# Two half gates computed between FFN-out and the mixing projection, and the transposes around them rearranged

## The chip, the cores and the metric

The kernel runs on one core of one Trainium2 chip, in a single launch. The metric is the device time of one execution in microseconds, taken as the median of several runs. A core has five engines with a queue each, which they work through in order: TensorE (PE in the profile; its weight loads are PEld), VectorE (DVE), ScalarE (ACT), GpSimd (POOL) and SyncE (SP), which here only issues loads. GpSimd issues the stores.

## The reference

One layer of an encoder, with x of 1024 tokens by 1024 features, all in fp32, DFF = 2816:

```python
x = x + 0.5 * post1(swiglu_1(pre1(x)))          # FFN1: (silu(x W_g) * (x W_u)) W_out
u = pre_mix(x)                                   # RMS norm with a gain
[rq|rk|rv|rg|nq|nk|nv|g_ret|g_na] = u @ W_mix_in # widths 512 512 1024 1024 512 512 512 1024 1024
y_ret = (silu(rg) * headnorm(retention(rq, rk, rv))) @ W_ret_out   # 4 heads, chunks of 128, both directions
y_na  = (neighbourhood_attention(nq, nk, nv) + bias) @ W_na_out
x = x + post_mix((sigmoid(g_ret) * y_ret + sigmoid(g_na) * y_na) @ W_mix_out)
x = x + 0.5 * post2(swiglu_2(pre2(x)))          # FFN2
```

The gates g_ret and g_na have 1024 features each, in eight blocks of 128.

## The kernel before

**Products.** Every fp32 operand is split into a rounded high part and a remainder (`split`: ScalarE casts the high part at L60, VectorE subtracts at L61; sometimes GpSimd subtracts). `mm3` then makes three matmuls, high by high, high by low and low by high, at L87, L88 and L89. A matmul has a 128x128 stationary operand and a 128x512 moving one. `load_w` loads a 512 KB block of weights into `wraw` and splits it into two pieces, `wh` and `wl`, so it costs two casts and two subtractions. Banks of PSUM come from two rings, `ps` with six and `pt` with two.

**Token tiles.** The 1024 tokens are eight tiles of 128. The large products (FFN and mixing projection) go by 2x2 blocks in seven products instead of eight, whose operands are blocks and sums of blocks of the transposed activations: a11, a12, a21, a22 and s1 to s4. Tiles 0 to 3 give a11 and a12; tiles 4 to 7 give a21, a22 and, together with a11 and a12, s1 to s4.

**FFN-out** (`ffn_out`) runs seven products of 11 steps, in each step four token tiles of `mm3` (12 matmuls). From the fifth product on, `later.pop(0)` puts one small piece of work of tiles 0 to 3 ahead of each step. First come eight entries that finish the second halves of the outputs (`more`, each followed by an empty one), then sixteen: four stages for each of four tiles, (0) the mean square and its power on GpSimd, (1) the residual update L493 and squares, (2) the power and the normalisation L504, (3) the transposes L126 (`flip`), which write into `ps` for tiles 0 and 1 (up to the end of the sixth product, a12) and into `pt` for the others. Before, the four stages of tile 0 come first, then those of tile 1, and so on, so the transposes are the entries 4, 8, 12 and 16 of the sixteen. Tile t's halves lie in `q`. Each `flip` ends in `put`, which reads the transposed bank and writes the split operands.

**Between FFN-out and the projection.** Tiles 4 to 7 are normalised at the end of FFN-out. Their transposes are interleaved by hand with filler work for TensorE, drawn step by step (one step is one `mm3`) from the generator `first()`: 32 steps of the v projection of attention (`vproj`, the matmuls `ps<-wh,a11h` and so on), then the 24 steps of `mx.leads()`, the first products of the mixing projection. FLIP_FILL is the number of steps before each of the four flips and, last, the number between a flip and the s4 split that belongs to it. Before it asks for 40 of 56 steps, and the rest is drained afterwards. For a tile of 4 to 7, `put` does the following ring. First half (g = 0): ScalarE copies the bank to `cmb` (a21, L272), VectorE forms s3 with L276 and L277. Second half (g = 1): ScalarE casts a22h and VectorE takes a22l from the bank, VectorE adds s1 (L282), casts and subtractions for s3, VectorE subtracts the bank for s2 (L284), casts and subtractions for s1 and s2, GpSimd L287 and L288 form s4, ScalarE casts s4h and GpSimd takes s4l. `cmb` has four buffers. The evictions of the filler's v banks are `ev<-ps` on ScalarE at L1120.

**The projection.** `mx.run` takes the jobs in order; the first needs s2 of all tiles (product `ps<-s2h,wh`), whose start waits for the copy at L376.

**Later fillers.** `products()` is the generator of fillers for attention and retention: 128 steps of the v projection of retention, then the gates g_na of blocks 4 to 7 (16 steps each, both halves of the tokens), the gates g_ret, and the output projection of attention: 384 steps in all. Attention takes 148 of them (NA_FILL) and retention 234 (RET_FILL), each at a place written out by hand; what is left is drained after retention. Retention runs four heads of eight chunks. For each chunk its last step is `store`: SyncE loads a block of rg (two buffers), TensorE transposes the normalised result (L946), VectorE multiplies (L947), GpSimd issues the store to `ry` (L67). After head 3, `ry` is loaded again, split into `xy` and multiplied by W_ret_out (`ps<-xy,wh`).

These lines draw and place the filler between FFN-out and the projection, and the later gates:

```python
FLIP_FILL = (8, 8, 8, 8, 2)
def first():
    yield from vproj(wnv, ((0, 1, 2, 3),), done_nv)
    yield from mx.leads()
for f, k in zip(rest, FLIP_FILL):
    fill(k)
    f = f()
    if f is not None:
        fill(FLIP_FILL[4])
        f()
```

Of the kernel before, what the change touches and what calls it, by code (L numbers as in the profile page):

```python
# [10 lines left out]
F32 = mybir.dt.float32  # L11
F32R = mybir.dt.float32r
AF = mybir.ActivationFunctionType
# [5 lines left out]
P = 128  # L19
D = 1024  # L20
S = 1024
KT = D // P
# [6 lines left out]

NA_FILL = (12, 2, 2)  # L30
RET_FILL = (14, 2, 2, 4, 2, 3, 0, 1, 2)
FLIP_FILL = (8, 8, 8, 8, 2)
NA_UNITS = ((0, 0, 0), (3, 1, 0), (1, 0, 1), (1, 0, 2), (4, 1, 1), (4, 1, 2), (2, 0, 3), (5, 1, 3))
KEY_OFF = (0, 8, 24, 32)
RET_SCALE = 128 ** -0.5
# [499 lines left out]
def ffn_out(c, q, blocks, junk, xtile, w_out, t_out, gl, ep, side={}):  # L535


    nc = c.nc
    NK = FT // 2
    tt = nc.vector.tensor_tensor  # L540
    later, rest, flips, xs = [], [], [], {}

    def xload(t):

# [23 lines left out]
    def p4(u, b):  # L568
        tt(q[3][:, u], b, q[3][:, u], ALU.add)
        ep.square(u, 0, q[3][:, u], b)  # L570
        later.extend(stages(u, (q[3][:, u], q[2][:, u])))

    def stages(t, halves):
        g = ep.steps(t, xs[t], halves)

        f = []
        return [lambda: next(g), lambda: next(g)] + [
            lambda: f.append(next(g)), lambda: f[0](*(("ps", 6) if i < 6 else ("pt", 2)))] * (ep.pre is not None)
# [47 lines left out]
    for n, (i, k) in enumerate(steps):  # L626
# [9 lines left out]
        if later and i > 3:  # L636
            f = later.pop(0)
# [372 lines left out]
def trunk_layer(ctx: ExitStack, tc, x, g1a, w1i, w1o, g1b, gma, wmt, wnv, wrv, logits, dtab, rope, bias,  # L1010
                wro, wno, wmo, gmb, g2a, w2i, w2o, g2b, out):
    nc = tc.nc
# [5 lines left out]
    c = Core(tc, const, wpool, psum, dram)  # L1018
# [4 lines left out]
    def dt(name, shape):  # L1023
        return dram.tile(shape, F32, name=name)
# [4 lines left out]
    d = {  # L1029
        "a21": dt("a21", [P, 4, 512]),  # L1030
        "nq": dt("nq", [NHP, P, S]), "nk": dt("nk", [NHP, P, S]), "nv": dt("nv", [16, 64, 512]), "nvg": dt("nvg", [4, 4, P, 512]),
        "no": dt("no", [NHP, P, S]), "rq": dt("rq", [RH, P, S]), "rk": dt("rk", [RH, P, S]),
        "rv": dt("rv", [TT, P, D]), "rg": dt("rg", [8, P, S]), "ry": dt("ry", [8, P, S]),
        "sr": dt("sr", [8, P, S]), "sn": dt("sn", [8, P, S]), "z": dt("z", [8, P, S]), "m": dt("m", [8, P, S]),
    }

    def rows(a):
        return lambda t: a[t * P:(t + 1) * P, :]
# [3 lines left out]
    def pool(stack, name, side="left"):  # L1042
        return stack.enter_context(tc.tile_pool(name=name, bufs=1, side=side, reuse_waits="tile"))
# [16 lines left out]
    with (tc.tile_pool(name="tw1", bufs=1, reuse_waits="tile") as tw,  # L1060
# [10 lines left out]
    ep = pool(ep_stack, "ep1", "right")  # L1071
    fo = Epilogue(c, ep, g1b, gma, rows(x), rows(x1), wx.put)
    q = [ep.tile([P, 4, 512], F32, tag="q", name="q", bufs=2) for _ in range(2)]
# [9 lines left out]
    rest = ffn_out(c, q, Blocks(c, (g0, g0, g0, g1), (3, 1)), junk,  # L1083
                   lambda t: (m1, m2, ep, ep)[t // 2].tile([P, D], F32, tag="xs", name="xs", bufs=2 + t // 4 * 2),
                   w1o, t1o, gl[0], fo,
                   {n: (lambda j=j: ahead.update({j: c.load_w(wnv[j])})) for j, n in enumerate((65, 66))})
# [8 lines left out]
    def xh(t, k):  # L1095

        return a21 if (t, k) == (1, 0) else wx.op(("a11", "a12", None, "a22")[2 * t + k])

    def vproj(src, groups, done):

        for toks in groups:
            banks = {t: c.bank() for t in toks}
            for k in range(KT):
                if k % 2 == 0:
                    w = ahead.pop(k // 2) if k // 2 in ahead else c.load_w(src[k // 2])
                for t in toks:
                    tt = slice((t % 4) * P, (t % 4 + 1) * P)
                    c.mm3(banks[t], [q[:, k % 4, tt] for q in xh(t // 4, k // 4)], w[k % 2], k == 0, k == KT - 1)
                    yield
            for t in toks:  # L1110
                done(t, banks[t])

    evpool = []

    def ev():
        return evpool[0].tile([P, S], F32, tag="ev", name="ev", bufs=3)
# [18 lines left out]
    jobs += [(32 + 2 * i, 33 + 2 * i, d["sn"][2 * i], d["sn"][2 * i + 1], AF.Sigmoid) for i in range(2)]  # L1135
    mx = Pairs(c, wx, [(wmt[j[0]], wmt[j[1]]) for j in jobs], 3)

    def first():
        yield from vproj(wnv, ((0, 1, 2, 3),), done_nv)
        yield from mx.leads()  # L1140

    fill = Filler(first())
    evpool[:] = [wx.tmp, None]
# [52 lines left out]
    mix.tile([P, 40], F32, name="pad")  # L1196
    evpool[:] = [mix]

    def gate(i, dst, halves=(0, 1)):

        w = c.load_w(wmt[i])
        e = ev()
        for h in halves:
            hs = slice(h * 512, (h + 1) * 512)
            b = c.bank()
            for k in range(KT):
                ks = slice((k % 4) * P, (k % 4 + 1) * P)
                c.mm3(b, [p[:, ks] for p in w[k // 4]], [q[:, k % 4] for q in xh(h, k // 4)], k == 0, k == KT - 1)
                yield
            nc.scalar.activation(e[:, hs], b, AF.Sigmoid)  # L1210
        hs = slice(halves[0] * 512, halves[-1] * 512 + 512)
        c.store(dst[:, hs], e[:, hs])

    def products():
        for j in range(2):
            yield from vproj(wrv[j], ((0, 1, 2), (3, 4, 5), (6, 7)), done_rv(j))
        yield "rv"
        for i in range(4, 8):
            yield from gate(32 + i, d["sn"][i])
        for i in range(4):  # L1220
            yield from gate(24 + i, d["sr"][i])
        for i in range(4, 8):
            yield from gate(24 + i, d["sr"][i], (1,))
        x1_stack.close()
        opool = pool(o_stack, "o", "right")
        oop = [opool.tile([P, 4, S], F32R, name=f"o{q}") for q in "hl"]
        for i in range(4, 8):
            raw = c.raw(d["no"][i - 4])
            c.split(oop[0][:, i - 4], oop[1][:, i - 4], raw)
            yield from gate(24 + i, d["sr"][i], (0,))  # L1230

        for i in range(8):
            if i % 2 == 0:
                w = c.load_w(wno[i // 2])
            e = ev()
            nc.sync.dma_start(e, d["sn"][i])
            for h in range(2):
                hs = slice(h * 512, (h + 1) * 512)
                b = c.bank()
                for k in range(4):  # L1240
                    c.mm3(b, [p[:, k * P:(k + 1) * P] for p in w[i % 2]], [q[:, k, hs] for q in oop], k == 0, k == 3)
                    yield
                nc.vector.tensor_tensor(e[:, hs], b, e[:, hs], ALU.mult)
            c.store(d["z"][i], e)
# [23 lines left out]
    for i0 in (0, 3, 6):  # L1268
        tiles = range(i0, min(i0 + 3, 8))
        m, z, w, banks = {}, {}, {}, {}  # L1270
# [16 lines left out]
        for i in tiles:  # L1287
            for k in range(KT if i0 > 0 else 0):
                one(i, k)
            for h in range(2):  # L1290
                hs = slice(h * 512, (h + 1) * 512)
# [33 lines left out]
    q = [op.tile([P, 4, 512], F32, tag="q", name="q", bufs=4) for _ in range(4)]  # L1325
# [86 lines left out]
```

## Time and profile before

| | |
|---|---|
| median of three runs | 2306.59 us (2305.39 to 2307.46) |
| profiled execution | 2306.69 us, its span 2304.8 us |
| granted TensorE clock, mean | 0.989 |
| instructions | 30361 |
| HBM read, written | 301.60 MB, 123.21 MB |

A row of the windows gives the stretch, its length, then busy time and number of instructions on PE, PEld, DVE, ACT and POOL, then the granted clock, the DMA engines' busy share and GB/s. A row of the waits gives who waits on which tile and line, for whom; then the total, the count and the longest in us. A row of the timeline gives start and duration in us, engine, line, operation, output and inputs, shapes, the count of merged instructions, and in brackets the idle time before it and what ended it. Line numbers are those of the kernel.

### The profile page before, as it was taken

How to read it: one execution, taken by the hardware profiler on the slowest of the kernel's cores; microseconds unless marked ns; L12 is line 12 of the kernel's file. 1: busy time of each engine (PE TensorE's matmuls, PEld its weight loads, DVE VectorE, ACT ScalarE, POOL GpSimd, SP SyncE). 2: the span in 40 equal slices, each digit the busy share in tenths (PEclk: the TensorE clock that was granted, in tenths of full speed). 3: DMA queues.
4: the chain of work that ended last, by engine and by line, in shares of the span. 5: the costliest groups of instructions: out<-in, count | busy, mean ns of one | idle time of the engine just before them, and what ended most of it. 6: DMA issues, size and time to landing. Idle time of an engine off the chain costs nothing.

```text
span 2304.8 us, 30361 instructions
## 1 busy us (share of the span) xinstructions
PE 2218.8 (96%) x10288; PEld 1839.6 (80%) x10288; DVE 1675.8 (73%) x2945; ACT 1003.4 (44%) x2102; POOL 593.1 (26%) x689
## 2 busy tenths in 40 slices
PE   6999999999998999999999999999799999998998
PEld 5788888778776877778888888887588888887886
DVE  7897777645778758869875688547897777774576
ACT  6333332244554322258885675225533322233453
POOL 5342423210124134411101222101534242421012
PEclk9999999999999999999999999999899999999999
DMA  5464545477654542257645577866555454546765
GB/s 177 153 205 147 178 144 176 153 231 227 207 192 142 178 165 96 110 185 238 220 161 178 163 222 235 291 213 204 173 172 187 151 173 146 174 138 213 233 199 185
DMA packets 163675, 422.63 MB, mean 183 GB/s; under 512 B 19712, under 2 KB 47488, under 8 KB 163456
## 3 DMA queue, kind: packets, MB, share of 16 engines
q1 hardware_dynamic: 130080, 310.04, 42.4%
q0 software_dynamic: 33440, 110.65, 12.4%
q8 instruction: 81, 1.33, 0.2%
q14 instruction: 74, 0.61, 0.1%
HBM read 301.60 MB, written 123.21 MB: 184 GB/s over the span
## 4 chain that ended last, share of the span: by engine, by line
PE 80%; DVE 11%; issue 3%; POOL 3%; DMA 1%; ACT 1%; SPq 0%; POOLq 0%; DVEq 0%; ACTq 0%
PE ps L89 25%; PE ps L87 24%; PE ps L88 24%; DVE wl L61 2%; PE pt L89 1%; PE pt L87 1%; PE pt L88 1%; POOL rstd L97 1%; PE ps L725 1%; PE pt L744 1%; POOL cmb L287 1%; DVE tmp L117 1%; DVE t L378 1%; POOL cmb L288 1%; DVE xs L493 1%
## 5 line engine op out<-in xcount | busy, mean ns | idle before, releaser
L61 DVE TENSOR_TENSOR wl<-wraw,wh 128x512 fp32r<-128x512 f32 x662 | 468.9, 728 | 80.4 <-ACT wh L60 79.4
L60 ACT CAST wh<-wraw 128x512 fp32r<-128x512 f32 x670 | 390.3, 618 | 218.2 <-PE ps L88 71.2
L87 PE MATMUL ps<-wh,gh 128*128 128x512 f32 x612 | 241.5, 396 | 19.2 <-ACT gh L60 18.1
L61 DVE TENSOR_TENSOR gl<-graw,gh 128x512 fp32r<-128x512 f32 (+2 forms) x178 | 124.3, 699 | 173.8 <-ACT gh L60 173.6
L88 PE MATMUL ps<-wl,gh 128*128 128x512 f32 x612 | 241.2, 395 | 2.1 <-DVE wl L61 2.1
L89 PE MATMUL ps<-wh,gl 128*128 128x512 f32 x612 | 240.1, 395 | 0.8 <-DVE gl L61 0.5
L60 ACT CAST gh<-graw 128x512 fp32r<-128x512 f32 (+2 forms) x178 | 107.1, 602 | 226.6 <-PE ps L88 87.4
L414 ACT ACTIVATE c<-c 128x512 f32<-128x512 f32 x88 | 55.7, 633 | 283.1 <-DVE c L384 198.5
L87 PEld LDWEIGHTS ps<-wh,gh 128*128 128x128 f32 x612 | 116.4, 190 | 45.9 <-ACT gh L60 19.7
L89 PEld LDWEIGHTS ps<-wh,gl 128*128 128x128 f32 x612 | 116.4, 191 | 28.2 <-DVE gl L61 4.0
L88 PEld LDWEIGHTS ps<-wl,gh 128*128 128x128 f32 x612 | 116.6, 191 | 26.8 <-DVE wl L61 3.2
L483 POOL TENSOR_TENSOR q<-q,gain 128x512 f32<-128x512 f32 x22 | 33.6, 1546 | 357.7 <-ACT ps L482 343.4
L60 ACT CAST wh<-t 128x512 fp32r<-128x512 f32 x58 | 36.1, 622 | 202.6 <-DVE t L378 184.5
L89 PE MATMUL ps<-a12h,wl 128*128 128x512 f32 x280 | 110.4, 394 | 3.7 <-DVE wl L61 3.7
L87 PE MATMUL ps<-a11h,wh 128*128 128x512 f32 x280 | 112.4, 401 | 1.4 <-ACT wh L60 0.7
L89 PE MATMUL ps<-a11h,wl 128*128 128x512 f32 x280 | 110.9, 396 | 0.7 <-DVE wl L61 0.7
L87 PE MATMUL ps<-a12h,wh 128*128 128x512 f32 x280 | 111.1, 397 | 0.0
L88 PE MATMUL ps<-a11l,wh 128*128 128x512 f32 x280 | 111.0, 397 | 0.0
L88 PE MATMUL ps<-a12l,wh 128*128 128x512 f32 x280 | 109.8, 392 | 0.0
L87 PE MATMUL ps<-a22h,wh 128*128 128x512 f32 x280 | 109.8, 392 | 0.0
L89 PE MATMUL ps<-a22h,wl 128*128 128x512 f32 x280 | 109.1, 390 | 0.0
L88 PE MATMUL ps<-a22l,wh 128*128 128x512 f32 x280 | 109.0, 389 | 0.0
(354 smaller groups left out, 5975.6 us busy)
## 6 DMA issues: line engine op xcount, KB each, us to landing
wraw<-in_dram SPq DMA_DIRECT2D x243, 512.0 KB, 4.4
tw<-in_dram SPq DMA_DIRECT2D x88, 256.0 KB, 3.3
t<-tw POOLq DMA_DIRECT2D x88, 256.0 KB, 4.2
wraw<-t SPq DMA_DIRECT2D x40, 512.0 KB, 3.6
g0s<-cmb POOLq DMA_DIRECT2D x44, 256.0 KB, 4.2
graw<-g0s SPq DMA_DIRECT2D x44, 256.0 KB, 2.8
g1s<-cmb POOLq DMA_DIRECT2D x44, 256.0 KB, 4.2
graw<-g1s SPq DMA_DIRECT2D x44, 256.0 KB, 2.7
```

The source lines that it names most:

```text
L60: nc.scalar.copy(h, src)
L61: (eng or nc.vector).tensor_tensor(l, src, hf, ALU.subtract)
L87: mm(ps, a[0], b[0], start=start, stop=False)
L88: mm(ps, a[0], b[1], start=False, stop=False)
L89: mm(ps, a[1], b[0], start=False, stop=stop)
L97: self.nc.gpsimd.tensor_tensor(r[:, :n], ms, self.mhalf[:, :n], ALU.pow)
L117: nc.vector.scalar_tensor_tensor(xn[:, bs], x[:, bs], r[:, 0:1], gain[:, bs], op0=ALU.mult, op1=ALU.mult)
L287: nc.gpsimd.tensor_tensor(s3, h2, s3, ALU.subtract)
L288: nc.gpsimd.tensor_tensor(s3, s3, l2, ALU.add)
L378: tt(t2, b22, t1, ALU.subtract)
L414: nc.scalar.activation(gate[j], gate[j], AF.Silu)
L483: (eng or c.nc.gpsimd).tensor_tensor(h if out is None else out, h, self.post[:, b * 512:(b + 1) * 512], ALU.mult)
```

## The change

Four edits. First, the first halves (tokens 0 to 511) of the g_na gates of blocks 4 and 5 (`EARLY`) move from `products()` into `first()`, between the v projection and the leads: 16 steps, 48 matmuls, each half closed by a sigmoid on ScalarE and a store. The second halves stay in `products()`, so that the weights of these two gates are loaded and split twice. `products()` then holds 368 steps, and attention and retention still ask for 382. Second, `gate` moves up to be known to `first()`; in the early place its result goes to a 512 wide tile of the pool `wx.tmp`. Third, FLIP_FILL asks for 52 of now 72 steps: 8, 12, 12 and 12 before the flips. Fourth, the sixteen entries of tiles 0 to 3 in FFN-out are skewed: tile n starts its first stage while tile n - 1 does its second and tile n - 2 its third, and the transposes are the entries 7, 11, 14 and 16 of the sixteen. FFN2's out product, which has no such transposes, keeps the old order. Lines move down by two at first, and by six or seven later (L126 is now L128, L60 is L62, L272 is L274, L946 is L952).

```diff
-FLIP_FILL = (8, 8, 8, 8, 2)
+EARLY = (4, 5)
+SKEW = [(t, j) for n in range(7) for t, j in ((n - 3, 3), (n - 2, 2), (n - 1, 1), (n, 0)) if 0 <= t < 4]
+FLIP_FILL = (8, 12, 12, 12, 2)
...
     def p4(u, b):
         tt(q[3][:, u], b, q[3][:, u], ALU.add)
         ep.square(u, 0, q[3][:, u], b)
-        later.extend(stages(u, (q[3][:, u], q[2][:, u])))
+        chains.append(stages(u, (q[3][:, u], q[2][:, u])))
+        if u == 3 and ep.pre is not None:
+            later.extend(chains[t][j] for t, j in SKEW)
+        elif u == 3:
+            later.extend(f for g in chains for f in g)
...
+    def gate(i, dst, halves=(0, 1)):
+        w = c.load_w(wmt[i])
+        n = len(halves) * 512
+        e = ev() if len(evpool) == 1 else evpool[0].tile([P, 512], F32, tag="ev", name="ev", bufs=4)
...
     def first():
         yield from vproj(wnv, ((0, 1, 2, 3),), done_nv)
+        for i in EARLY:
+            yield from gate(32 + i, d["sn"][i], (0,))
         yield from mx.leads()
...
         for i in range(4, 8):
-            yield from gate(32 + i, d["sn"][i])
+            yield from gate(32 + i, d["sn"][i], (1,) if i in EARLY else (0, 1))
```

On ScalarE, around the flips of tiles 5, 6 and 7 between FFN-out and the projection, the queue before reads as follows; L272 is the copy of a tile's first half, `ev` the eviction of a v bank, s4h the last cast of a tile's ring. The first row here is the copy of tile 6, the last that of tile 7.

```order
L272 COPY cmb<-pt 128x512
L60 CAST a22h<-pt 128x4x128
L1120 COPY ev<-ps 128x512 x4
L60 CAST s4h<-cmb 128x4x128
L60 CAST s3h<-cmb 128x4x128
L60 CAST s1h<-cmb 128x4x128
L60 CAST s2h<-cmb 128x4x128
L272 COPY cmb<-pt 128x512
```

The same place after the change, from the s4h of tile 5 to the s4h of tile 6; `wh<-wraw` are the weights of the early gates, L1155 is their sigmoid, and `wh<-t_6525` is a weight of the first lead.

```order
L62 CAST s4h<-cmb 128x4x128
L274 COPY cmb<-pt 128x512
L62 CAST a22h<-pt 128x4x128
L62 CAST wh<-wraw 128x512
L62 CAST s3h<-cmb 128x4x128
L62 CAST wh<-wraw 128x512
L62 CAST s1h<-cmb 128x4x128
L1155 ACT_TABLE_LOAD
L1155 ACTIVATE ev<-ps 128x512
L62 CAST s2h<-cmb 128x4x128
L62 CAST wh<-t_6525 128x512
L62 CAST s4h<-cmb 128x4x128
```

Before, the copy and the a22h cast of tile 6 stood ahead of the s4h of tile 5; now tile 6's copy stands behind it, four weight and gate instructions have come in between, and the next rows (a second sigmoid, a weight cast, then the copy of tile 7) stand behind the s4h of tile 6.

On TensorE, at the end of head 3 of retention, the queue before: `ps<-vh,ah` and `ps<-sfh,qh` are the last chunk's products, L946 a result's transposes, and `ps<-oh,wh` filler from the output projection of attention.

```order
L87 MATMUL ps<-vh,ah 128x256
L88 MATMUL ps<-vl,ah 128x256
L89 MATMUL ps<-vh,al 128x256
L87 MATMUL ps<-sfh,qh 128x256
L88 MATMUL ps<-sfl,qh 128x256
L89 MATMUL ps<-sfh,ql 128x256
L946 MATMUL pt<-ident,yn 128x128 x2
L87 MATMUL ps<-oh,wh 128x512
L88 MATMUL ps<-ol,wh 128x512
L89 MATMUL ps<-oh,wl 128x512
```

The same place after, as far as the first products of W_ret_out (`ps<-xy,wh`):

```order
L89 MATMUL ps<-vh,ah 128x256
L90 MATMUL ps<-vl,ah 128x256
L91 MATMUL ps<-vh,al 128x256
L89 MATMUL ps<-sfh,qh 128x256
L952 MATMUL pt<-ident,yn 128x128 x2
L90 MATMUL ps<-sfl,qh 128x256
L91 MATMUL ps<-sfh,ql 128x256
L952 MATMUL pt<-ident,yn 128x128 x4
L89 MATMUL ps<-xy,wh 128x512 x6
L90 MATMUL ps<-xy,wh 128x512
```

The filler groups `ps<-oh,wh` that stood between the last chunks and their transposes are gone from here: the generator has run out.

More of the change, by code (lines that the diff above doesn't have):

```diff
@@ L540, in ffn_out @@
     tt = nc.vector.tensor_tensor
-    later, rest, flips, xs = [], [], [], {}
+    later, rest, flips, xs, chains = [], [], [], {}, []
     def xload(t):
@@ L1136, in trunk_layer @@
     mx = Pairs(c, wx, [(wmt[j[0]], wmt[j[1]]) for j in jobs], 3)
+    def gate(i, dst, halves=(0, 1)):
+        w = c.load_w(wmt[i])
+        n = len(halves) * 512
+        e = ev() if len(evpool) == 1 else evpool[0].tile([P, 512], F32, tag="ev", name="ev", bufs=4)
+        for j, h in enumerate(halves):
+            b = c.bank()
+            for k in range(KT):
+                ks = slice((k % 4) * P, (k % 4 + 1) * P)
+                c.mm3(b, [p[:, ks] for p in w[k // 4]], [q[:, k % 4] for q in xh(h, k // 4)], k == 0, k == KT - 1)
+                yield
+            nc.scalar.activation(e[:, j * 512:(j + 1) * 512], b, AF.Sigmoid)
+        c.store(dst[:, halves[0] * 512:halves[0] * 512 + n], e[:, :n])
     def first():
         yield from vproj(wnv, ((0, 1, 2, 3),), done_nv)
+        for i in EARLY:
+            yield from gate(32 + i, d["sn"][i], (0,))
         yield from mx.leads()
@@ L1197, in trunk_layer @@
     evpool[:] = [mix]
[L1199 to L1212, printed above, removed]
     def products():
```

## Prediction

> **What bounds the kernel now.** I read the page's first part, then the windows around the edited places, the waits of TensorE there, and the timelines of the five engines.
>
> ```profile
> PE 2218.8 (96%) x10288; PEld 1839.6 (80%) x10288; DVE 1675.8 (73%) x2945; ACT 1003.4 (44%) x2102; POOL 593.1 (26%) x689
> 617.00:667.00 50.00, 45.84 (x214) 37.38 (x213) 43.63 (x69) 30.22 (x69) 17.47 (x16) 1.00 0.73 236
> 683.00:742.00 59.00, 50.64 (x229) 40.70 (x227) 53.55 (x77) 30.86 (x64) 31.17 (x29) 0.97 0.39 131
> 1433.00:1449.00 16.00, 16.00 (x93) 13.89 (x92) 10.15 (x25) 8.87 (x20) 6.34 (x10) 1.00 0.46 163
> ```
>
> TensorE is the bound nearly everywhere. The edit touches three stretches: 617 to 667 (first four tiles normalised and transposed inside FFN-out), 683 to 742 (last four tiles), and the end of retention at 1433 to 1449, where TensorE has no idle time at all. In the second stretch TensorE loses 8.4 us, and VectorE is busy 53.55 of 59 us: it is the denser engine there. Who TensorE waits for from 617 to 742:
>
> ```profile
> PE pt L126 <- ACT cmb L272: 3.4, 1, 3.4
> PE pt L126 <- DVE cmb L284: 3.4, 2, 2.4
> PE ps L126 <- DVE q L504: 2.3, 1, 2.3
> PE pt L126 <- ACT pt L482: 1.9, 1, 1.9
> PE ps L87 <- ACT ev L376: 0.8, 1, 0.8
> ```
>
> Third and fourth rows are in the first stretch, the rest in the second. In the timeline:
>
> ```profile
> 626.04 0.39 PE L89 MATMUL pt<-wh,gl 128*128 128x512 f32 x1
> 628.70 0.52 PE L126 MATMUL ps<-ident,q 128*128 128x128 f32 x3 [2.27 <-DVE q L504]
> 643.24 0.39 PE L88 MATMUL pt<-wl,gh 128*128 128x512 f32 x1
> 654.12 0.39 PE L88 MATMUL ps<-wl,gh 128*128 128x512 f32 x1
> 656.37 1.27 PE L126 MATMUL pt<-ident,q 128*128 128x128 f32 x8 [1.86 <-ACT pt L482]
> 691.94 1.03 PE L126 MATMUL pt<-ident,q 128*128 128x128 f32 x8
> 692.73 0.48 PE L87 MATMUL ps<-wh,a11h 128*128 128x512 f32 x1
> 722.95 0.63 PE L126 MATMUL pt<-ident,q 128*128 128x128 f32 x4 [2.39 <-DVE cmb L284]
> 724.24 0.63 PE L89 MATMUL ps<-a12h,wl 128*128 128x512 f32 x1
> 724.66 0.63 PE L87 MATMUL ps<-a12h,wh 128*128 128x512 f32 x1
> 738.26 0.50 PE L87 MATMUL ps<-s2h,wh 128*128 128x512 f32 x1 [0.83 <-ACT ev L376]
> ```
>
> Forty-eight matmuls start from 643.24 up to 654.12, so one takes 0.227 us start to start; 48 is also what the two moved half gates hold, so the moved work is 10.9 us. In place of that pace the first two gaps took 628.70 - 626.04 - 0.23 = 2.43 us and 656.37 - 654.12 - 0.23 = 2.02 us.
>
> **Part one, the skew.** The transposes of tiles 0, 1 and 2 move 36, 36 and 16 matmuls later (8.2, 8.2 and 3.6 us), tile 3's stay. Tile 0 then comes 5.7 us after its data, tile 2 needs the bank that it waited 2.0 us for and comes 3.6 us later. No instruction is added, and VectorE keeps its 43.63 us; over 45.6 us that is 96%, so it is tight, and I assume that the weight splits stay ahead of their use. Both gaps go: -4.45 us. Bound: if VectorE's order makes the second one stay, -2.4; no better than -4.45, as nothing else waits there.
>
> **Part two, the last four tiles.** Each transposed tile goes round a ring: ScalarE copies a21, VectorE does eight operations, GpSimd two, ScalarE casts s4h. The first job's s2 product waits for the end of tile 7's ring. Before:
>
> ```profile
> 701.51 0.69 DVE L276 TENSOR_TENSOR cmb<-a11h,cmb 128x512 f32<-128x512 f32 x1
> 705.11 0.68 DVE L276 TENSOR_TENSOR cmb<-a11h,cmb 128x512 f32<-128x512 f32 x1
> 705.72 0.68 DVE L284 TENSOR_TENSOR cmb<-pt,cmb 128x512 f32<-128x512 f32 x1
> 715.03 0.68 DVE L276 TENSOR_TENSOR cmb<-a11h,cmb 128x512 f32<-128x512 f32 x1
> 724.52 0.68 DVE L276 TENSOR_TENSOR cmb<-a11h,cmb 128x512 f32<-128x512 f32 x1
> 732.94 0.68 DVE L61 TENSOR_TENSOR s2l<-cmb,s2h 128x512 fp32r<-128x512 f32 x1
> 733.70 1.67 POOL L287 TENSOR_TENSOR cmb<-a12h,cmb 128x512 f32<-128x512 f32 x1 [3.63 <-DVE s2l L61]
> 737.10 0.62 ACT L60 CAST s4h<-cmb 128x512 fp32r<-128x512 f32 x1 [2.91 <-POOL cmb L288]
> 737.63 0.58 ACT L376 COPY ev<-ps 128x512 f32<-128x512 f32 x1
> 710.12 1.77 DVE L61 TENSOR_TENSOR wl<-wraw,wh 128x512 fp32r<-128x512 f32 x1
> 709.73 1.61 POOL L288 TENSOR_TENSOR cmb<-cmb,a12l 128x512 f32<-128x512 f32 x1
> 1206.82 1.28 ACT L1210 ACT_TABLE_LOAD   x1
> 1208.12 0.60 ACT L1210 ACTIVATE ev<-ps 128x512 f32<-128x512 f32 x1
> ```
>
> Tiles 4 to 7 begin (L276) at 701.51, 705.11, 715.03 and 724.52, about 9.5 us apart, VectorE being dense at 0.60 us per operation (705.11 to 705.72) and slower beside GpSimd (1.77 against 0.68). From tile 7's s2l to the s2 product it is 738.26 - 732.94 = 5.3 us. Between the first L276 and that s2l VectorE has 42 operations before and 51 now: two weights are loaded a second time, which is four splits more (2.4 us bare, up to 7.1 us at 1.77), and five operations of the first job come ahead. Worse is ScalarE's order, shown under the change: the copies of tiles 6 and 7 now stand behind s4h of tiles 5 and 6, so two rings no longer overlap there. Laying after's queues on these durations, on before's clock: tile 4's ring from 701.5; tile 5 from 708.3 with s2l at 716.2; GpSimd's pair, with stores between, until 721.1; s4h 0.62 and the copy 0.58 let tile 6 begin at 722.4; its last read of PSUM ends at 727.9; table load 1.28 and sigmoid 0.60 pass in front of s2h, s2l ends 729.7; GpSimd until 733.1; s4h, the second sigmoid, a weight cast and the copy, 0.6 each, so tile 7 begins at 735.7; ten operations put s2l's end at 741.9; the pair, s4h and L376 as before give s2 at 746.7. TensorE alone would reach it at 743.3: from 691.94 it has 145 + 48 matmuls (43.8 us) and 32 transposes (eight take 692.73 - 691.94 = 0.79, so 3.2), and by the same queues waits 3.7 us in tile 5, whose second half needs tile 4's last PSUM read (705.72 + 0.68), and 0.7 in tile 7. So s2 starts 8.4 us later, with 10.9 us more work done: a gain of 2.5 us. Ends: 0.6 us later if TensorE never waits (the gain is then 10.3), 10.9 later if every microsecond of the added work shows. I take 8.4, the value the queues give. From its start to that of the activation behind it a table load takes 1208.12 - 1206.82 = 1.30 us. The Trainium skill, "ScalarE: Activation LUTs", What ACT_TABLE_LOAD costs, has about 2.66 us for a switch with its drain; no gap here is as long: the row gives 1.30, and the measurement decides; by the page s2 would be at 748.1 and the whole 1.4 us longer.
>
> Later the first Silu of the projection needs its table again: up to 1.3 us on ScalarE, which is not dense there; I take 0. Retention and attention get the same number of TensorE fillers as before until they run out; two table loads inside attention go. I take 0.
>
> **Part three, the end of retention.** The filler held 384 steps for 382 asked; now it holds 368, so the last 16 (10.9 us) are missing exactly in the last two chunks. What is late next:
>
> ```profile
> 1433.17 0.28 PE L87 MATMUL ps<-vh,kdh 128*128 128x256 f32 x1
> 1449.21 0.62 PE L87 MATMUL ps<-xy,wh 128*128 128x512 f32 x2
> 1436.26 0.42 DVE L947 TENSOR_TENSOR rg<-pt,rg 128x256 f32<-128x256 f32 x1
> 1443.53 0.42 DVE L947 TENSOR_TENSOR rg<-pt,rg 128x256 f32<-128x256 f32 x1 [0.32 <-PE pt L946]
> 1445.17 0.56 POOL L97 TENSOR_TENSOR rstd<-ss,mhalf 128x1 f32<-128x1 f32 x1 [0.21 <-DVE ss L935]
> 1445.77 0.51 ACT L937 ACTIVATE yn<-y,rstd 128x256 f32<-128x256 f32 x1 [0.94 <-POOL rstd L97]
> 1446.18 2.93 ACT L60 CAST xy<-wraw 128x1024 fp32r<-128x1024 f32 x3
> ```
>
> From chunk 5's update (1433.17) to the first product of the retention output (1449.21) it is 16.04 us: 10.9 filler and 5.1 retention's own. Without filler a ring of two gate buffers decides: gate product (L947), store, reload, product two chunks on. It took 1443.53 - 1436.26 = 7.3 us. Chunk 3's product can come at 2.2 us after the update, so chunk 5's at 8.4 (6.2 us on; part of the 7.3 was waiting). Behind it on VectorE stands chunk 7's ss, so its rstd ends at 10.3, yn at 10.85, the first xy cast at 11.9: TensorE resumes at 11.95 instead of 16.04. Of 10.9 us taken away 4.1 come back; 6.8 are new idle time. Ends: all 10.9 come back, or none.
>
> **The clock.** After the 2.39 us wait at 722.95 the matmuls at 724.24 and 724.66 are 0.42 us apart, half pace, nine of them: 1.8 us. After the longer wait for L272's copy, 3.4 us, I see none. The new idle places (3.4 us before s2, 6.8 in the tail) could cost 1.8 us each; I count one.
>
> **Sum.** -4.45 + 8.44 - 4.09 + 1.8 = +1.7 us on 2306.69, the profiled execution, which is 0.1 us from the median: 2308.3 us.
>
> **Rivals.** *The rings stay overlapped* (faster): if GpSimd's pairs end early enough, or VectorE has room, s2 starts when TensorE gets there without waiting, 0.6 us later and not 8.4: 2308.3 - 7.8 = 2300.5. For it: 145 matmuls before, 193 now, over the same rings. Against: ScalarE takes its queue in order, and s4h stands in front of the copy. It decides below 2302 when 6.3 of the 7.8 us are won. *The gate ring holds the tail* (slower): if the product of chunk 5 comes as late as it did (7.3 us after chunk 3's, and chunk 3's no earlier), the xy products start at 16.0 us as before and nothing comes back: 2308.3 + 4.1 = 2312.4. For it: VectorE is in order and the wait for the reload stands in front of the last normalisation. Against: chunk 3's product waited in a queue that loses its filler work. Slower by over 0.2% needs 2.9 of the 4.1 us. *Half pace twice*: both idle stretches followed by nine slow matmuls, 2310.1; the two rows at 724 are for it, the fast pace after L272's 3.4 us against. The Trainium skill, "TensorE: Matmul & The Clock Gate", Why this matters for your kernels, asks for no idle gap over about 3 us, or the clock halves; by that both would, though here 3.4 us did not and 2.39 did.
>
> **Chances.** A difference of about 0.2%, 4.6 us, is what a measurement of this kernel can tell from no change, so faster begins below 2302.0 and slower above 2311.2. Forecast 0.36, of which 0.06 ends below and 0.08 above, since two of its terms (8.4 and 4.1) come out of queues laid by hand; overlapped rings 0.26 (0.20 below); gate ring 0.28 (0.20 above); half pace twice 0.10 (0.04 above). Faster 0.26, same 0.42, slower 0.32. The range begins at 2298.7, the first rival without the clock charge (its wait before s2 is gone), and ends at 2316: the second rival with the second half-pace period (1.8) and the second gap of part one back (2.0) is 2316.2. The forecast's own range, over the ends of the tail, is 2301.5 to 2312.4.
>
> **What would show it.** Right: no wait at the transposes of tiles 0 and 2; ScalarE's copies of tiles 6 and 7 behind s4h, L276's successors about 14 and 13 us apart; s2 about 4 us later than 738.26 on the new clock; 6 to 7 us of TensorE idle between chunk 5's update and the first xy product. Wrong: a dense TensorE from 680 to the s2 product, a tail without idle time, or new waits in attention or in retention's earlier heads, for which I count nothing.

## The result and the profile after

| | before | after |
|---|---|---|
| median of 14 runs | 2306.20 us (2304.50 to 2309.05) | 2313.32 us (2309.52 to 2317.21) |
| ratio, 95% interval | | 1.0030 (1.0022 to 1.0038) |
| profiled execution, span | 2306.69, 2304.8 us | 2310.03, 2308.2 us |

The changed kernel is 7.1 us slower, 5.0 us above the forecast of 2308.3 and inside its range. The execution that was profiled is the second fastest of the 14, 3.3 us under their median, so its trace shows less than half of the loss as a total. Its stages show where it lies. First the busy times of the page, then the windows of the edited places (columns as before):

```profile
PE 2219.6 (96%) x10288; PEld 1838.5 (80%) x10288; DVE 1677.5 (73%) x2949; ACT 1006.5 (44%) x2106; POOL 595.7 (26%) x691
617.00:667.00 50.00, 47.68 (x220) 39.37 (x219) 44.88 (x71) 31.13 (x72) 19.19 (x16) 0.97 0.75 237
683.00:742.00 59.00, 55.41 (x254) 46.00 (x253) 53.55 (x78) 32.91 (x65) 28.02 (x29) 0.97 0.42 142
1336.00:1345.00 9.00, 7.14 (x40) 5.80 (x39) 6.48 (x14) 7.60 (x17) 2.60 (x4) 1.00 0.49 141
1435.00:1452.50 17.50, 13.40 (x81) 10.87 (x79) 11.58 (x36) 10.23 (x29) 7.24 (x12) 0.90 0.33 115
```

The first stretch still holds 2.3 us of idle TensorE, the second only 3.6, and VectorE is as busy there as before, 53.55 of 59 us. New are the third (1.9 us idle at the start of retention's head 2, in the midst of a stage that was dense) and the fourth, the end of retention (4.1 us).

The next table cuts the profiled executions of all kernels at the same instructions of TensorE. Its columns are, in us: from a given FFN-out matmul (614.03 us before) to the first filler of the v projection; from there to the first s2 product; to the first update of retention (`ps<-vh,kdh`); to chunk 5's update in head 3; to the first xy product; to the last xy product. Kernels with the same work there differ by up to 4 us in the third column, and by 2 to 3 us in the stretches that are not shown (the start, and all that follows the last xy). In the profiled pair the stages shown add up to +5.7 us, the others to -2.4.

| kernel | FFN-out | flips, to s2 | to first update | to chunk 5 | to xy | xy |
|---|---|---|---|---|---|---|
| before | 72.47 | 51.76 | 482.81 | 212.10 | 16.04 | 86.82 |
| after | 71.71 | 59.70 | 479.30 | 217.33 | 11.07 | 88.58 |
| difference | -0.76 | +7.94 | -3.51 | +5.23 | -4.97 | +1.76 |
| forecast | -4.45 | +8.44 | 0 | 0 | -4.09 | +1.8 (clock) |
| e1 skew alone | 75.23 | 52.13 | 482.27 | 212.76 | 16.04 | 86.81 |
| e2 all but the skew | 72.48 | 59.70 | 480.93 | 218.55 | 11.09 | 88.76 |
| e3 before, first fill 30 | 72.48 | 51.75 | 493.11 | 216.61 | 11.01 | 89.29 |
| e4 after, first fill 0 | 71.96 | 59.71 | 477.83 | 211.45 | 14.67 | 91.31 |
| e5 after, old flip order | 71.77 | 61.42 | 483.34 | 217.34 | 10.95 | 89.42 |
| e6 skew, tile 1 earlier | 71.35 | 52.16 | 481.65 | 213.55 | 16.13 | 86.82 |
| e7 after, four rg buffers | 70.69 | 59.68 | 482.00 | 218.38 | 10.51 | 89.59 |
| e8 two entries moved | 70.45 | 51.78 | 483.01 | 213.37 | 16.04 | 86.81 |
| e9 after, 12 2 2 1 | 70.81 | 59.74 | 477.61 | 207.27 | 14.67 | 90.18 |
| e10 after, GpSimd splits | 70.43 | 63.56 | 479.51 | 218.88 | 10.97 | 88.63 |
| e11 e8's order, 12 2 2 0 | 70.49 | 59.95 | 480.99 | 205.52 | 17.44 | 87.23 |
| e12 e8's order, 8 2 2 1 | 70.16 | 59.66 | 476.54 | 204.93 | 17.43 | 87.50 |

Three of the forecast's terms stand within 1 us of what was measured: the flips, the tail, the clock. Two do not: the skew won 0.8 us and not 4.45, and retention before its tail, costed at nothing, lost 5.2. The third column, also costed at nothing, is 3.5 us shorter, which is within its spread.

**FFN-out.** The waits of TensorE from 617 to 760 and the place of the new one (timeline of TensorE, ScalarE and VectorE):

```profile
PE pt L128 <- DVE cmb L286: 3.6, 1, 3.6
PE ps L89 <- DVE a11l L63: 2.3, 1, 2.3
PE ps L89 <- ACT ev L378: 1.6, 1, 1.6
652.97 0.50 PE L89 MATMUL ps<-wh,gh 128*128 128x512 f32 x1 [2.32 <-DVE a11l L63]
654.14 0.63 PE L90 MATMUL ps<-wl,gh 128*128 128x512 f32 x1
654.57 0.63 PE L91 MATMUL ps<-wh,gl 128*128 128x512 f32 x1
649.49 0.58 ACT L62 CAST a11h<-ps 128x512 fp32r<-128x512 f32 x1
649.82 0.69 DVE L63 TENSOR_TENSOR gl<-graw,gh 128x512 fp32r<-128x512 f32 x1
651.63 0.69 DVE L63 TENSOR_TENSOR wl<-wraw,wh 128x512 fp32r<-128x512 f32 x1
652.23 0.68 DVE L63 TENSOR_TENSOR a11l<-ps,a11h 128x512 fp32r<-128x512 f32 x1
```

Both old waits (for q and for pt) are gone. But the skew puts tile 1's transposes ahead of the last step of the sixth product, in two banks of the ring `ps`, and the seventh product takes four banks of that ring. Two of them are free: six matmuls go on without a wait. The first matmul on the third bank, at 652.97, waits until VectorE has read the transposed bank, and VectorE does four operand splits first (649.82 to 652.23). Then seven matmuls go at 0.43 us each.

**The flips.** VectorE's first operation of each tile, tile 7's s2l, and what follows (timeline):

```profile
700.07 0.68 DVE L278 TENSOR_TENSOR cmb<-a11h,cmb 128x512 f32<-128x512 f32 x1
706.68 0.68 DVE L278 TENSOR_TENSOR cmb<-a11h,cmb 128x512 f32<-128x512 f32 x1
720.53 1.40 DVE L278 TENSOR_TENSOR cmb<-a11h,cmb 128x512 f32<-128x512 f32 x1 [0.61 <-ACT cmb L274]
734.20 0.68 DVE L278 TENSOR_TENSOR cmb<-a11h,cmb 128x512 f32<-128x512 f32 x1
739.77 0.69 DVE L63 TENSOR_TENSOR s2l<-cmb,s2h 128x512 fp32r<-128x512 f32 x1
743.59 0.62 ACT L62 CAST s4h<-cmb 128x512 fp32r<-128x512 f32 x1 [3.33 <-POOL cmb L290]
744.75 0.50 PE L89 MATMUL ps<-s2h,wh 128*128 128x512 f32 x1 [1.61 <-ACT ev L378]
```

This execution reaches the place 1.44 us ahead of the one before. With that, the forecast's 701.5, 708.3, 722.4, 735.7, 741.9 and 746.7 become 700.1, 706.9, 721.0, 734.3, 740.5 and 745.3. The fifth is the end of tile 7's s2l, which came at 740.46: the queues laid by hand were right to 0.6 us.

**Retention.** First the low part of the attention output's split (`ol`) in the trace before, then the same in the trace after with what stands behind it, and TensorE:

```profile
1350.90 1.23 DVE L61 TENSOR_TENSOR ol<-wraw,oh 128x1024 fp32r<-128x1024 f32 x1 [0.31 <-ACT oh L60]
...
1342.10 1.23 DVE L63 TENSOR_TENSOR ol<-wraw,oh 128x1024 fp32r<-128x1024 f32 x1 [0.56 <-ACT oh L62]
1343.97 0.75 DVE L63 TENSOR_TENSOR vl<-vraw,vh 128x256 fp32r<-128x256 f32 x2
1344.44 0.39 PE L90 MATMUL ps<-vl,kdh 128*128 128x256 f32 x1 [1.63 <-DVE vl L63]
```

The waits of TensorE of more than 0.2 us from retention's start to the xy products, where there were none:

```profile
PE pt L952 <- ACT yn L943: 3.6, 3, 2.5
PE ps L90 <- DVE vl L63: 1.6, 1, 1.6
PE ps L89 <- DVE y L937: 0.7, 1, 0.7
```

Of the 5.2 us that are lost ahead of chunk 5, 2.3 lie at this vl. The rest is a wait of 0.7 us for y at 1369 and delays of up to 0.3 us each in heads 2 and 3, whose cause stays open. The tail, from chunk 5's update to the first xy product, took 11.07 us (11.95 forecast, 16.04 before):

```profile
1441.38 0.28 PE L89 MATMUL ps<-vh,kdh 128*128 128x256 f32 x1
1450.12 0.69 PE L952 MATMUL pt<-ident,yn 128*128 128x128 f32 x2 [2.47 <-ACT yn L943]
1452.45 2.92 PE L89 MATMUL ps<-xy,wh 128*128 128x512 f32 x6 [0.25 <-ACT xy L62]
```

The generator of filler does not only hold matmuls. Between its gates it loads and splits the attention output, four pieces of a 1.05 us cast and a 1.22 us subtraction. With 16 steps gone from its front, every place in retention gets what stood 16 steps further on. These splits left a place behind the backward updates and came to the first of them, where TensorE needs each chunk's vl at once. That the waits come from this shift is what the third experiment shows; that the wait for vl is due to these splits, and not to other work of those 16 steps, is read from VectorE's queue and was not tested apart.

### The profile page after: what moved, and what is told of

Read it like the earlier page. It is cut to its first block, busy times and chain, and to the rows that moved or that the text cites. A ratio compares the mean times of both kernels' runs of the same rounds, so it can differ in the third digit from the quotient of the medians.

```text
span 2308.2 us, 30380 instructions
## 1 busy us (share of the span) xinstructions
PE 2219.6 (96%) x10288; PEld 1838.5 (80%) x10288; DVE 1677.5 (73%) x2949; ACT 1006.5 (44%) x2106; POOL 595.7 (26%) x691
## 5 line engine op out<-in xcount | busy, mean ns | idle before, releaser
L63 DVE TENSOR_TENSOR wl<-wraw,wh 128x512 fp32r<-128x512 f32 x666 | 470.3, 725 | 70.4 <-ACT wh L62 69.3
L62 ACT CAST wh<-wraw 128x512 fp32r<-128x512 f32 x674 | 393.1, 618 | 224.5 <-PE ps L90 76.9
L62 ACT CAST gh<-graw 128x512 fp32r<-128x512 f32 (+2 forms) x178 | 106.8, 602 | 224.2 <-PE ps L90 83.9
L62 ACT CAST wh<-t 128x512 fp32r<-128x512 f32 x58 | 36.1, 622 | 205.7 <-DVE t L380 196.1
```

The costliest lines, as they stand in the source:

```text
L62: nc.scalar.copy(h, src)
L63: (eng or nc.vector).tensor_tensor(l, src, hf, ALU.subtract)
```

## The experiments

Each kernel is timed against the kernel before on one chip; the ratio has its 95% interval.

**e1: the skew alone.**

```diff
-EARLY = (4, 5)
+EARLY = ()
-FLIP_FILL = (8, 12, 12, 12, 2)
+FLIP_FILL = (8, 8, 8, 8, 2)
```

> Only the skew of the sixteen entries; no early gates, FLIP_FILL as before. Theory, from the trace after: the two old gaps go, but tile 1's transposes now come at the end of the sixth product and hold a ps bank that the seventh product's first bank needs, with the eviction behind weight splits on VectorE: a new wait of 2.3 us for a11l and slow matmuls behind it, so 0.8 us are won of 4.45, about 2305.4 against 2306.2. Rival, the forecast: both gaps go and nothing takes their place, 2301.8.

Measured: 2305.16 us (2303.07 to 2310.79, 11 runs), before 2306.49; ratio 1.0001 (0.9992 to 1.0010). The forecast's 4.5 us lie outside the interval, a gain of up to 1.8 us inside. The times fall into two groups, six up to 2305.2 and five from 2307.1 on; the profiled one (2309.96) is of the second. Its timeline:

```profile
655.85 0.79 PE L89 MATMUL ps<-wh,gh 128*128 128x512 f32 x1 [4.76 <-DVE a11l L63]
649.15 0.62 ACT L62 CAST wh<-wraw 128x512 fp32r<-128x512 f32 x1 [2.38 <-DMA wraw<-in_dram]
```

The new wait took 4.8 us and not 2.3: ScalarE stood 2.4 us for a weight load, and VectorE's splits, and a11l behind them, came later by as much. The skew has made a place where the landing of a load is passed on to TensorE; a single trace may show it at 2.3 us or at twice that.

**e2: everything but the skew.**

```diff
-            later.extend(chains[t][j] for t, j in SKEW)
+            later.extend(f for g in chains for f in g)
```

> Everything but the skew: early gates and the new FLIP_FILL, the old order of the sixteen entries. Theory: the whole loss is here, 7 to 8 us over before, 2313 to 2314.5; the s2 product starts some 8 us later than before and retention from its first update to the first xy product takes as long as before (228 us) with 10.9 us less filler. Rival, the forecast's skew of 4.45 us: without it 2313.3 + 4.45 = 2317.8.

Measured: 2313.45 us (2311.12 to 2316.64, 6 runs), ratio 1.0034 (1.0022 to 1.0045). The whole loss lies in the early gates with their fill counts; the skew takes nothing measurable off it. Retention, from the first update to xy, took 229.64 us and not 228: with 10.9 us of filler less it is no shorter.

**e3: the kernel before, with retention's first fill of 30.**

```diff
-RET_FILL = (14, 2, 2, 4, 2, 3, 0, 1, 2)
+RET_FILL = (30, 2, 2, 4, 2, 3, 0, 1, 2)
```

> The kernel before with one number changed: the first filler of retention asks for 30 steps and not 14. No work is added or taken away; the generator is 16 steps further on at every later place and runs out 14 steps early, as it does after the change. Theory: retention's own loss shows alone: the operand splits of attention's output fall on the start of head 2, the last two chunks have no filler, 11 us over before (2317). Rival, the forecast's tail: idle time only in the tail, 6.8 us (2313). If the gate ring holds it: 10.9 us from the tail alone, with no wait at the start of head 2.

Measured: 2318.21 us (2316.56 to 2320.52, 5 runs), ratio 1.0056 (1.0042 to 1.0070), that is 11.7 us over before with no work added. Waits of TensorE from 1210 on:

```profile
PE pt L946 <- ACT yn L937: 3.9, 3, 2.5
PE ps L88 <- DVE vl L61: 1.6, 1, 1.6
PE ps L87 <- DVE y L931: 0.8, 1, 0.8
```

They are the three waits of the changed kernel, to 0.3 us, without any early gate. The 16 steps cost 10.3 us where they were put. The tail (11.01 us) gave 5.0 of them back, about as the forecast had it, but the stretch ahead of chunk 5 lost 4.5, so that from the first update to xy only 0.5 us came back. The xy stretch, with slow matmuls at its start, took 2.5 us more.

**e4: the changed kernel with no first fill.**

```diff
-RET_FILL = (14, 2, 2, 4, 2, 3, 0, 1, 2)
+RET_FILL = (0, 2, 2, 4, 2, 3, 0, 1, 2)
```

> The changed kernel with the first filler of retention at 0 and not 14, so that 368 steps are asked of 368, and the last chunks have their filler. Theory: the waits at the start of head 2 and in the tail go, since every later place gets what it got before: if the head of retention can do without its 14 steps, 217 us from the first update to the first xy product and 2302; if all of their 9.5 us are needed there, 2311.6. Rival: the loss lies ahead of attention alone, 2313.

Measured: 2311.24 us (2310.08 to 2314.17, 8 runs), ratio 1.0025 (1.0015 to 1.0035). The stretch to chunk 5 is back at 211.45 us and the tail full, as expected; the 217 us of the text mixed up the stretches, since the first fill lies ahead of the first update. What was won went at the two ends:

```profile
PE ps L90 <- DVE xy L63: 2.8, 1, 2.8
PE pt L900 <- DVE kdl L66: 1.5, 1, 1.5
PE pt L900 <- DMA kraw<-rk: 1.0, 1, 1.0
```

The start of retention waits for its load and the first splits without filler. At its end nothing is left to drain, and the first xy products wait 2.8 us for their split, which two drained steps had covered before.

**e5: the changed kernel with the flips' old order.**

```diff
-FLIP_FILL = (8, 12, 12, 12, 2)
+FLIP_FILL = (9, 8, 8, 8, 2)
```

> The changed kernel with FLIP_FILL at 9, 8, 8, 8, 2, so that most of the early gates' steps come behind the last flip and ScalarE's copies of tiles 6 and 7 stand again ahead of the s4 casts of tiles 5 and 6, as in the kernel before. Work, loads and the later filler are those of the changed kernel. Theory of the rings in series (the forecast): the order of ScalarE is what delays s2, and with the old order s2 comes as soon as TensorE is done with its own work, 3 to 4 us earlier, so 2309 to 2310. Rival, VectorE is dense there and the order counts for nothing: s2 at the same place, 2313.

Measured: 2313.23 us (2311.41 to 2320.39, 6 runs), ratio 1.0030 (1.0017 to 1.0042): no gain. The profiled execution is the longest of the six, so its stages are read and not its total. The rings did overlap (tile 7 begins at 724.85, some 10 us earlier than in the changed kernel, counted from the first filler), but s2 came no earlier, and the waits moved:

```profile
PE pt L128 <- DVE cmb L286: 3.5, 2, 2.4
PE pt L128 <- ACT cmb L274: 3.1, 1, 3.1
...
724.85 1.76 DVE L278 TENSOR_TENSOR cmb<-a11h,cmb 128x512 f32<-128x512 f32 x1
```

TensorE now waits 6.6 us at tiles 5 to 7, where the changed kernel waits 3.6 us and then 1.6 us ahead of s2, which follows at once here. Tile 7's last cast s4h ends at 739.8 here, 7.4 us ahead of s2 at 747.2, so s2 waits for TensorE and not for the ring. The forecast's order of ScalarE is what happens in the changed kernel, and undoing it wins nothing: with the rings in series or overlapped, TensorE's own work and its waits for tile after tile take about as long.

**e6: the skew alone, tile 1's transposes one step earlier.**

```diff
-... (2, 1), (3, 0), (1, 3), (2, 2) ...
+... (2, 1), (1, 3), (3, 0), (2, 2) ...
```

> Only the skew, with one entry moved: tile 1's transposes one step (12 matmuls, 2.7 us) earlier, ahead of tile 3's first stage, so that their bank is evicted before the seventh product asks for it. Theory: the wait for a11l of 2.3 to 4.8 us goes or shrinks by up to 2.7 us, 2302 to 2304 against 2306.2. Rival: the eviction waits for VectorE, whose queue is as full one step earlier, and the wait stays: 2305.

Measured: 2305.42 us (2302.40 to 2307.51, 11 runs), before 2306.41; ratio 0.9997 (0.9988 to 1.0006). The edit is shown against the order of e1, cut to the entries that move. The wait was still there:

```profile
PE ps L89 <- DVE a11l L63: 1.9, 1, 1.9
```

The transposes began 3.0 us earlier than in the changed kernel (642.57 against 645.53), their eviction a11l only 0.6 (651.59 against 652.23): ScalarE's cast a11h came at 648.92, behind casts of weights whose load had landed late (ScalarE idle for 2.2 us up to 643.79), and a11l then stood behind VectorE's queue. So the rival names a part of it, and the larger part lies on ScalarE. The times don't separate theory and rival.

**e7: the changed kernel with four buffers for rg.**

```diff
-rg = spool.tile([P, 2, P], F32, tag="rg", name="rg", bufs=2)
+rg = spool.tile([P, 2, P], F32, tag="rg", name="rg", bufs=4)
```

> The changed kernel with four buffers for the gate rg in retention instead of two. Theory (the gate ring holds the tail): loads no longer wait for the store two chunks before, the product behind the reload no longer stands in front of the last normalisation's work on VectorE, and the xy products start 2 to 4 us earlier: 2309.5 to 2311. Rival: the tail's idle time is the chain of the last chunk itself (product, normalisation, transposes), the ring counts for nothing: 2313.

Measured: 2314.80 us (2312.06 to 2316.02, 5 runs), ratio 1.0035 (1.0022 to 1.0047). The tail took 10.51 us and not 11.07, with this wait in it:

```profile
PE pt L952 <- ACT yn L943: 3.2, 2, 2.5
```

The ring is worth half a microsecond. What holds the tail is then the last chunks' own chain of product, normalisation and transposes, as the wait that stays says; no run shortens that chain.

**e8: before, with two of the sixteen entries moved.**

```diff
-(0, 2), (0, 3), (1, 0), (1, 1), ... (2, 2), (2, 3), (3, 0), (3, 1), (3, 2), (3, 3)
+(0, 2), (1, 0), (0, 3), (1, 1), ... (2, 2), (3, 0), (3, 1), (2, 3), (3, 2), (3, 3)
```

> The kernel before with two of the sixteen entries of FFN-out moved and nothing else: tile 0's transposes one entry later (behind tile 1's first stage), tile 2's two entries later (behind tile 3's first two stages). Tile 1's transposes stay where they were, so no ps bank is held late. Theory: both old gaps go (2.4 and 2.0 us) and no wait for a11l takes their place, 2301.5 to 2302 against 2306.3. Rival: VectorE has its 96% there in any order, its late splits hold TensorE at another place, 2305.

Measured: 2304.38 us (2301.09 to 2308.80, 11 runs), before 2305.32; ratio 0.9995 (0.9986 to 1.0004). In the three traces with this order (e8, e11, e12) the FFN-out stretch took 70.2 to 70.5 us, 2.0 to 2.3 less than before; in the seven with the full skew 70.4 to 75.2. The waits in e8's trace:

```profile
PE pt L128 <- ACT pt L484: 1.2, 1, 1.2
PE pt L128 <- DVE a11l L63: 0.9, 1, 0.9
```

The edit above gives the order of the entries, which the kernel before does not spell out, with the unchanged ones left out. The wait for q is gone; that for the bank is smaller, and tile 3 now waits for a bank of tile 2. Half of the 4.45 us is to be had, too little for these runs to show as a time.

**e9: the changed kernel with three steps less per head.**

```diff
-RET_FILL = (14, 2, 2, 4, 2, 3, 0, 1, 2)
+RET_FILL = (12, 2, 2, 1, 2, 3, 0, 1, 2)
```

> The changed kernel with RET_FILL starting 12, 2, 2, 1 and not 14, 2, 2, 4: three filler steps less ahead of each head's first chunk and two less at the start, so that 368 are asked of 368 and the last chunks have theirs again. Theory, filler is cover: at each of these places TensorE now waits for the splits of k, q, v and the states, up to 2.0 us a head, and the tail's loss of some 5 us (idle time and slow matmuls) is traded for up to 8; 2310 to 2314. Rival, only the tail needs cover and the moved 10.9 us come back as time: 2304 to 2306.

Measured: 2305.61 us (2303.88 to 2307.38, 11 runs), ratio 0.9996 (0.9987 to 1.0005). The rival's time was right: 7.7 us of the changed kernel's 2313.32 come back with two numbers. The longest wait of TensorE from 1210 to 1470 is this one; two others, for ah and for a gate's eviction, make 2.1 us together:

```profile
PE ps L90 <- DVE xy L63: 3.0, 1, 3.0
```

Ahead of each head's first chunk one step is nearly cover enough: the stretch to chunk 5 is 10.1 us shorter than in the changed kernel, of which 8.2 are the twelve steps that are gone from it, and the waits of 2.1 us are what that costs. The xy wait of e4 is here too, as nothing is left to drain.

**e10: the early gates' low parts on GpSimd.**

```diff
-        w = c.load_w(wmt[i])
+        w = c.load_w(wmt[i], nc.gpsimd if halves == (0,) and len(evpool) == 2 else None)
...
```

> The changed kernel with the four low parts of the early gates' weights subtracted on GpSimd and not on VectorE, nothing else changed. Theory, VectorE is the dense engine ahead of s2: its 2.4 to 5 us go, the rings come earlier, s2 1 to 2 us earlier, 2311.5 to 2312.5 against 2313.3. Rival: GpSimd stands in the rings too (its pair and the stores), so its four operations of some 1.6 us make them later, 2314 to 2317.

Measured: 2316.14 us (2313.02 to 2317.52, 5 runs), ratio 1.0043 (1.0029 to 1.0057). The lines left out hand the engine through `load_w` to its two splits. The rival's time was right, its reason only in part. One wait of TensorE took the whole cost, and its source lies ahead of the rings:

```profile
PE pt L128 <- DVE cmb L286: 8.4, 1, 8.4
696.96 8.06 DVE L506 SCALAR_TENSOR_TENSOR q<-xs,rstd,gain 128x512 f32<-128x512 f32 x4 [0.44 <-POOL rstd L99]
698.16 4.98 POOL L63 TENSOR_TENSOR wl<-wraw,wh 128x512 fp32r<-128x512 f32 x4
```

GpSimd did its four subtractions one after the other (1.25 to 1.29 us each), and one of VectorE's last normalisations, which ran beside them, took 6.06 us, where the others take 0.75. So tile 4's ring began at 704.94, 4.9 us later than in the changed kernel. It is VectorE that GpSimd's work held up, and not GpSimd's own place in the rings.

**e11 and e12: early gates, two entries moved, four steps kept for the drain.**

```diff
-RET_FILL = (14, 2, 2, 4, 2, 3, 0, 1, 2)
+RET_FILL = (12, 2, 2, 0, 2, 3, 0, 1, 2)    # e11
+RET_FILL = (8, 2, 2, 1, 2, 3, 0, 1, 2)     # e12
```

> The changed kernel with the order of FFN-out in which only tile 0's and tile 2's transposes move, and RET_FILL starting 12, 2, 2, 0: 364 steps are asked of 368, so that four are left for the drain after retention. Theory: against the run with 12, 2, 2, 1 (2305.6) the wait of 3.0 us for the first xy split is covered by 2.7 us of drained filler, and the order in FFN-out wins 1 us more; each head's lost step costs up to 0.7 us if cover is short there: 2301 to 2303.5. Rival, a step less per head is one too few: 2305 to 2307.

> The same with RET_FILL starting 8, 2, 2, 1: the four drained steps come from the head of retention and not from the four heads. Theory: at the head of retention 14 steps covered 8.5 of 9.5 us, so four fewer cost up to 2.7 us there and win what the other variant wins: 2302 to 2304.5. Rival: the first steps at that place are spare (two were), only the last ones are cover, 2301 to 2302.

Measured: e11 2303.70 us (2299.65 to 2308.61, 11 runs), ratio 0.9994 (0.9985 to 1.0003); e12 2302.77 us (2299.37 to 2307.25, 12 runs), ratio 0.9991 (0.9982 to 0.9999); before 2305.68. In e12 all waits of TensorE from 1200 to 1470 are these:

```profile
PE ps L89 <- DVE y L937: 0.5, 1, 0.5
PE ps L90 <- DVE xy L63: 0.4, 1, 0.4
PE ps L89 <- ACT ev L1155: 0.3, 1, 0.3
```

The xy wait is covered, and the first steps of retention's head were partly spare. e12 is the fastest kernel here, 10.6 us under the changed one and 2.9 under before. Its interval against before ends at 0.9999, hardly short of no change, and it is the best of twelve variants, so that this last gain is not shown.

## Why the prediction was right and wrong

The direction and the range held. The chance of 0.42 went to no measurable change; it was slower by 0.3%, which had 0.32. By its steps:

- **The skew (-4.45, bound -2.4).** Wrong in size, beyond its bound of -2.4. The step that failed is that the sum took the two gaps as won and put nothing for a wait in their place ("nothing else waits there", which was so in the order before): which ring the transposes' banks come from was known, and who asks for the next banks of that ring was not looked up. The two waits went as forecast, but a wait of 2.3 us in the pair, and of 4.8 in e1, in another place took what they gave: 0.8 us in the profiled pair, and e1's time is that of before.
- **The flips (+8.44).** Right in size, measured +7.94, and +7.9 to +8.2 in the six other kernels with the new FLIP_FILL and the splits on VectorE. The mechanism is weaker than the text has it. ScalarE's order did put the rings in series, but e5 undid that and won nothing.
- **Retention before its tail (0).** Wrong, and the largest miss: +5.2 us in the pair, +4.5 to +6.8 in e2, e3, e5, e7 and e10. The failed step is "get the same number of TensorE fillers as before until they run out". The number is the same, the content is not, and the content has splits on VectorE in it. In e2, e5, e7 and e10 the wait for vl was followed by six matmuls at half pace, in the pair and in e3 by none. The text named new waits in retention's earlier heads as what would prove it wrong.
- **The tail (-4.09).** Right in size, -4.97, and by luck: the text lets "a ring of two gate buffers" decide, and with four buffers (e7) the tail is 0.56 us shorter and no more. Of the 10.9 us taken away 5.9 did not come back: 4.1 us of idle time, where 6 to 7 were forecast, and the rest smaller delays. The rival of the gate ring gave 2312.4, close to the time, by the same ring, which e7 refutes.
- **The clock (+1.8).** Right as a sum, by luck: the xy stretch is 1.76 us longer, with the first matmuls after the tail's idle time at half pace. The 1.6 us wait ahead of s2 was followed by none, the new wait in FFN-out by seven slow matmuls that the text could not count. Which wait is followed by half pace, the last section says.
- **Attention (0).** Open. The changed kernel and its relatives with the same fills (e2, e5, e7, e10) took 479.3 to 483.3 us to the first update, the kernels without early gates and with the same fills 481.7 to 483.0. Two table loads less could be worth something there, but the spread from one kernel to the next is as large, and no run takes them out alone.

With means over kernels with the stage unchanged in place of the pair's values (for the skew and the flips, over those named with them) the sum is -0.7 + 7.9 - 1.4 + 5.2 - 5.1 + 2.2 = +8.1 us, and +7.1 was measured. The overlapped rings (2300.5) would have needed TensorE free of other waits, which e5 shows it is not.

## What to carry to other kernels

Filler drawn from one generator is a budget, and what is taken from its front is missing at its end and shifts everything between, side work included: after such a move, lay out anew which step falls where, and first look for the places that have more cover than they need (here three of four steps ahead of each head). When a transposition or any other short use of a bank is moved, ask who takes the next banks of that ring, and when. In a stretch where an engine is 90% busy, ask where a wait that goes may come back: here, the next place where that engine's results were asked for.

## What the runs showed of the hardware

The granted clock in the traces tells which wait is followed by half pace. It changes only on a grid of 3.41 us that runs through a whole execution. Two neighbouring slots of this grid in the trace after, around the wait ahead of 652.97, and two in the trace before, around the 3.4 us wait ahead of 704.59:

```profile
650.42:653.83 3.41, 1.09 (x6) 0.72 (x5) 3.41 (x7) 0.65 (x2) 0.00 (x0) 1.00 0.86 263
653.83:657.24 3.41, 3.41 (x10) 2.67 (x9) 2.95 (x5) 3.09 (x10) 2.29 (x2) 0.50 0.50 186
699.55:702.96 3.41, 1.62 (x10) 1.00 (x7) 2.98 (x6) 0.00 (x0) 0.59 (x1) 1.00 0.19 77
702.96:706.38 3.42, 1.79 (x10) 1.58 (x11) 3.42 (x7) 2.22 (x4) 0.74 (x1) 1.00 0.32 46
```

In the first slot TensorE is idle for 2.3 us, and the whole second slot has half the clock. In the trace before, the longer wait is cut by the grid into 1.8 and 1.6 us of idle time, and the clock stays. The same wait in e1 put 2.3 us into one slot, and two slots at half clock followed, with ten slow matmuls. In all 14 traces, the first 20 us and the end left out, a slot at full clock with less than 1.6 us of idle time was never followed by a slot at half clock, one with more than 1.8 us always was, and between the two both occur. So a wait of 2 us can cost some 1 to 2.5 us more (0.2 us for each slow matmul), or nothing, by where it falls on the grid. The Trainium skill, "TensorE: Matmul & The Clock Gate", Why this matters for your kernels, puts the limit at gaps of over about 3 us. These runs show the loss from 1.6 us of idle time in one slot on. A table load in the midst of the flips (724.85 in the trace after) took 1.28 us, began when the cast ahead of it ended, and the sigmoid followed 1.29 us after its start, as the rows before had it; no drain is seen. In e10 one operation of VectorE that takes 0.75 us elsewhere took 6.06 us, while GpSimd did four subtractions of 4.98 us together.
